# Regrouping channels by block copies from GpSimd's queue in the S5 and convolution mixer

## The chip, the cores and the metric
One core of one Trainium2 chip runs the whole kernel, a two-layer encoder trunk on 512 tokens of width 1024. The metric is the device time of one execution in microseconds (us), the median of several runs.

## The reference
Each layer is a mixer, a cross-attention and a gated FFN, each added to `h`. The change lies in the mixer of the second layer; the rest is the same. Cut to that:

```python
def s5_scan(u, ...):                       # u (B, S, G, Hc): 32 groups of 16 channels, 64 complex states
    bu_re = jnp.einsum('gph,bsgh->bsgp', bb_re, u)
    bu_im = jnp.einsum('gph,bsgh->bsgp', bb_im, u)
    _, _, s_re, s_im = lax.associative_scan(combine, (a_re, a_im, bu_re, bu_im), axis=1)
    return (jnp.einsum('ghp,bsgp->bsgh', c_re, s_re)
            - jnp.einsum('ghp,bsgp->bsgh', c_im, s_im))

def conformer_conv(h, conv_w, conv_b, ln_g, ln_b):
    val, gate = jnp.split(h, 2, axis=-1)
    u = depthwise_conv(val * jax.nn.sigmoid(gate), conv_w, conv_b)      # 31 taps
    return jax.nn.silu(layernorm(u, ln_g, ln_b))

def mixer_cd(hn, ...):
    u_c, h_d = split_sizes(hn @ w_in, (C_WIDTH, 2 * D_WIDTH))           # 512 and 2 x 512 channels
    u = u_c.reshape(Bn, S, C_NGROUPS, C_GROUP)
    y_f = s5_scan(u, ...); y_b = flip(s5_scan(flip(u), ...))
    z = jax.nn.gelu((y_f + y_b).reshape(Bn, S, C_WIDTH) + d_skip * u_c)
    o_c = z * jax.nn.sigmoid(z @ w_glu + b_glu)
    return jnp.concatenate([o_c, conformer_conv(h_d, ...)], axis=-1) @ w_out
```

## The kernel before
Activations lie with channels on the partitions: a tile is 128 channels by 512 steps. Projections are exact to f32: `mm3` (L206 to L208) runs three passes of 128x128 weights over 512 columns. Each weight block of 512 KB is loaded by SP (`wraw`, L147, three buffers `wr`), its high half made by ACT (`wh`, L201), its low half by DVE (`wl`, L202).

`mixer_cd` works on four blocks i = 0 to 3 of 128 channels, that is 8 groups each. Its stages and their letters:
- `u`, `v`, `g`: the projections to the scan's input, the convolution's value and its gate. `u_` evicts on DVE (L1327); the gate's product is L1447.
- `a`, `b`: `chunks` and `steps_` regroup a block. The 512 steps are 64 chunks of 8; eight transposes (L1336) put chunks on the partitions, ACT copies (L1337), eight more (L1345) put (step in chunk, channel of group) on the 128 partitions and (group, chunk) along the row, and ACT copies into `Rg` (L1353). `A`, `B` do the same for the convolution's input of the blocks 2 and 3, into `vg`.
- `l`, `L`, `m`, `w`: SP's loads of tables; `L` loads the two rotation tables `cst` of a block (L1363, two buffers, one for each direction).
- `c`, `C`: the scan of a block forward and backward: matmuls (L1374), ACT copy `T1` (L1377), two DMAs on SP that swap its halves (L1378, L1379), then on DVE the rotation (L1380 to L1382), the scan (L1384 or L1386) and the rotation back (L1387, L1388), whose last product frees the table's buffer.
- `s`, `x`, `y`: a second swap of halves on SP (L1394, L1395), the sum `xp` on DVE (L1402), and the output matmuls (L1416, L1418).
- `f`: `channels`, eight transposes (L1425) back to channels, the skip term on DVE (L1431, read with a stride from PSUM) and Gelu on ACT.
- `q`: two of the 30 taps of the convolution on DVE (L1463), for the blocks 0 and 1. For the blocks 2 and 3 `Z` does it by matmuls with tables (L1489), and `F` returns them by `channels` (L1497).
- `k`: a step of the next cross-attention's memory projections; `N` the sums of the layer norm.

The order of work is written out by hand in the string `CD` (L82 to L87), a letter and a block for each stage. `pinned` (L184) ties the first instruction of each stage on PE and on SP to that order; a scheduler places all else, so that the order on DVE follows from its choices:

```python
PS_ = (PE, nc.sync)
for st_ in CD.split():
    engs, fn = stage[st_[0]]
    pinned(engs, fn, int(st_[1]))
```

Of the kernel before, what the change touches and what calls it, by code (L numbers as in the profile page):

```python
# [90 lines left out]
def trunk(ctx, tc, xT, memT, pos, vec, amask, cmask, bmask,  # L91
# [1166 lines left out]
    def mixer_cd(norm, nnext, kv):  # L1258
# [70 lines left out]
        def chunks(src):  # L1329

            us = src.rearrange("p (c t) -> p t c", t=8)
            at = k4([64, 8, 8, 16], "at", 3)
            for hf in range(2):
                tp = tp_ps()
                for t in range(4):
                    PE.transpose(tp[:64, 128 * t:128 * t + 128], us[:, 4 * hf + t], ident)  # L1336
                A.activation(at[:, :, 4 * hf:4 * hf + 4].rearrange("c g t k -> c t g k"),  # L1337
                             tp[:64].rearrange("c (t g k) -> c t g k", t=4, k=16), AF.Copy)
            return at

        def steps_(at):

            rp = sc_ps()
            for g in range(8):
                PE.transpose(rp[:, 64 * g:64 * g + 64], at[:, g].rearrange("c t k -> c (t k)"), ident[:64, :64])  # L1345
            return rp
# [18 lines left out]
        def c_(i, d):  # L1365
# [44 lines left out]
        def y_(i):  # L1410
            At[i] = k4([64, 8, 8, 16], "at", 3)
            for hf in range(2):
                yp = sc_ps()
                for g in range(4):
                    o, gg = yp[:64, 128 * g:128 * g + 128], 4 * hf + g
                    PE.matmul(o, Rg[i][:, 64 * gg:64 * gg + 64], cm[i][0][:, gg], start=True, stop=False)  # L1416
                    for d in range(2):
                        PE.matmul(o, X[i, d][:, gg, d:d + 64], cm[i][1 + d][:, gg], start=False, stop=d == 1)  # L1418
                A.activation(At[i][:, :, 4 * hf:4 * hf + 4].rearrange("c t g k -> c g t k"),
                             yp[:64].rearrange("c (g t k) -> c g t k", g=4, k=16), AF.Copy)  # L1420

        def channels(at):
            yq = sc_ps()
            for t in range(8):
                PE.transpose(yq[:, 64 * t:64 * t + 64], at[:, t].rearrange("c g k -> c (g k)"), ident[:64, :64])  # L1425
            return yq

        def f_(i):
            us = uT[i].rearrange("p (c t) -> p t c", t=8)
            yq = channels(At[i])  # L1430
            V.scalar_tensor_tensor(us, us, vc("s5_d", i), yq.rearrange("p (t c) -> p t c", t=8),  # L1431
                                   op0=ALU.mult, op1=ALU.add)
            A.activation(uT[i], uT[i], AF.Gelu_apprx_tanh)

# [7 lines left out]
        def g_(i):  # L1442
            ps = half1(8 + i)
            g = b2("dg", 1)
            V.tensor_tensor(g, ps, R, ALU.mult)
            A.activation(g, g, AF.Tanh, scale=0.5)
            V.scalar_tensor_tensor(dv[i], g, 1.0, dv[i], op0=ALU.add, op1=ALU.mult)  # L1447

# [17 lines left out]
        def ca_(i):  # L1466
            Bt[i] = chunks(dv[i])

        def cb_(i):
            A.activation(vg[i % 2][:, :, 2:66], g3(steps_(Bt[i])), AF.Copy)  # L1470

# [10 lines left out]
        def z_(i):  # L1482
            hf = zs[i] = zs.get(i, -1) + 1
            if hf == 0:
                Bt[i] = k4([64, 8, 8, 16], "at", 3)
            yp, ts = sc_ps(), [cts.pop(0) for _ in range(2)]
            for g in range(4):
                for j in range(5):
                    PE.matmul(yp[:64, 128 * g:128 * g + 128], vg[i % 2][:, 4 * hf + g, j:j + 64], ts[g // 2][:, g % 2, j],  # L1489
                              start=j == 0, stop=j == 4)  # L1490
            A.activation(Bt[i][:, :, 4 * hf:4 * hf + 4].rearrange("c t g k -> c g t k"),
                         yp[:64].rearrange("c (g t k) -> c g t k", g=4, k=16), AF.Copy)

# [41 lines left out]

        PS_ = (PE, nc.sync)
        stage = {"u": (PS_, u_), "a": (PS_, a_), "b": (PS_, b_), "x": ((), x_), "y": (PS_, y_),
                 "l": (PS_, l_), "L": (PS_, r_), "m": (PS_, m_), "s": (PS_, s_),
                 "c": (PS_, lambda i: c_(i, 0)), "C": (PS_, lambda i: c_(i, 1)),
                 "f": (PS_, f_), "v": (PS_, lambda i: half0(4 + i)), "V": (PS_, v_),  # L1540
                 "g": (PS_, lambda i: half0(8 + i)), "G": (PS_, g_),
                 "A": (PS_, ca_), "B": (PS_, cb_), "w": (PS_, w_), "Z": (PS_, z_), "q": ((V,), q_), "F": (PS_, cf_), "N": (PS_, n_),
                 "k": (PS_, k_), "K": (PS_, lambda i: kv.load())}
# [102 lines left out]
def layout(inp):  # L1646
# [87 lines left out]
```

## Time and profile before

| | us |
|---|---|
| three runs: median (lowest to highest) | 1602.35 (1599.77 to 1603.43) |
| the profiled execution | 1605.85 |
| its span | 1604.1 |
| PE busy | 1558.4 (97%) |
| DVE busy | 1072.0 (67%) |
| ACT busy | 707.6 (44%) |
| GpSimd (POOL) busy | 327.3 (20%) |

The profile shows one execution. Its own time stands 1.75 us above its span and 3.5 us above the median of the runs. PE, DVE, ACT, POOL and SP are TensorE, VectorE, ScalarE, GpSimd and SyncE; SPq is SP's queue of DMAs. Busy shares over the whole span mix stages with different limits; the mixer in question lies between about 866 and 1110 us.

### The profile page before, as it was taken

Reading aid. Unit: us, or ns where it says so; the run is one execution under the profiler, and the core shown is the slowest. Engines: PE = TensorE matmul, PEld = TensorE weight load, DVE = VectorE, ACT = ScalarE, POOL = GpSimd, SP = SyncE. Lnnn points to the kernel's source line nnn. Section 1 sums busy time; section 2 is a strip of 40 time slices with the busy share of each in tenths; the row PEclk is TensorE's granted clock in tenths of the full one; section 3 lists DMA queues with packets and bytes.
Section 4 is the critical chain, followed back from the end, with each engine's and each line's share of the span. In section 5 each row is a group of like instructions: output and inputs, shape, how many; then the busy total and the mean of one; then the engine's idle time right before and its main releaser. Section 6 shows DMA issues by size and latency. Waiting matters only on the chain.

```text
span 1604.1 us, 20956 instructions
## 1 busy us (share of the span) xinstructions
PE 1558.4 (97%) x8036; PEld 1303.9 (81%) x8036; DVE 1072.0 (67%) x1492; ACT 707.6 (44%) x1089; POOL 327.3 (20%) x354
## 2 busy tenths in 40 slices
PE   9999999999999998998999998999999999999997
PEld 6787889888888776786788877888888888888887
DVE  7586766467568789479846797476646766636644
ACT  5464755355444344233336343374535444424423
POOL 8402000000049953553520000000000111100101
PEclk9999999999999999999999999999999999999998
DMA  5323333231222334544545666453202232332331
GB/s 179 109 65 94 110 114 106 79 118 57 76 73 94 120 116 122 168 125 128 149 151 202 210 223 224 157 184 107 90 27 92 94 103 93 96 101 92 95 104 65
DMA packets 76117, 189.11 MB, mean 118 GB/s; under 512 B 8368, under 2 KB 27440, under 8 KB 76016
## 3 DMA queue, kind: packets, MB, share of 16 engines
q1 hardware_dynamic: 75376, 186.58, 36.1%
q8 instruction: 63, 1.03, 0.3%
q0 software_dynamic: 320, 1.05, 0.2%
q14 instruction: 38, 0.31, 0.1%
q10 hardware_dynamic: 320, 0.13, 0.0%
HBM read 162.43 MB, written 19.01 MB: 113 GB/s over the span
## 4 chain that ended last, share of the span: by engine, by line
PE 70%; DVE 13%; POOL 6%; DMA 4%; ACT 3%; issue 3%; SPq 1%; ACTq 0%; DVEq 0%; POOLq 0%
PE mm L206 20%; PE mm L208 20%; PE mm L207 20%; DVE wl L202 2%; PE mm L737 2%; PE sc L1489 1%; DVE t L972 1%; DMA T1s<-T 1%; DVE t L971 1%; PE tp L724 1%; DVE t L976 1%; POOL t L1139 1%; PE sc L208 1%; PE sc L206 1%; PE sc L207 1%
## 5 line engine op out<-in xcount | busy, mean ns | idle before, releaser
L201 ACT ACTIVATE wh<-wr 128x1024 fp32r<-128x1024 f32 (+1 forms) x229 | 239.0, 1045 | 428.4 <-PE mm L207 311.3
L208 PE MATMUL mm<-hg,wl 128*128 128x512 f32 x1000 | 392.9, 393 | 15.9 <-DVE wl L202 15.9
L206 PE MATMUL mm<-hg,wh 128*128 128x512 f32 x1000 | 396.9, 397 | 1.3 <-ACT wh L201 1.3
L207 PE MATMUL mm<-hg,wh 128*128 128x512 f32 x1000 | 391.3, 391 | 0.0
L202 DVE TENSOR_TENSOR wl<-wr,wh 128x1024 fp32r<-128x1024 f32 (+1 forms) x229 | 296.2, 1294 | 76.4 <-ACT wh L201 74.4
L208 PEld LDWEIGHTS mm<-hg,wl 128*128 128x128 f32 x1000 | 189.0, 189 | 60.3 <-DVE wl L202 19.8
L206 PEld LDWEIGHTS mm<-hg,wh 128*128 128x128 f32 x1000 | 189.2, 189 | 42.9 <-issue 2.2
L207 PEld LDWEIGHTS mm<-hg,wh 128*128 128x128 f32 x1000 | 189.1, 189 | 39.5 <-issue 1.2
L976 POOL TENSOR_TENSOR t<-t,t 128x512 f32<-128x512 f32 x22 | 28.9, 1315 | 626.7 <-ACT t L182 622.7
L208 PE MATMUL mm<-g,wl 128*128 128x512 f32 x324 | 126.7, 391 | 2.7 <-DVE wl L202 2.7
L206 PE MATMUL mm<-g,wh 128*128 128x512 f32 x324 | 126.9, 392 | 0.0
L207 PE MATMUL mm<-g,wh 128*128 128x512 f32 x324 | 126.2, 389 | 0.0
L968 DVE TENSOR_TENSOR u<-mm,R 128x512 f32<-128x512 f32 x88 | 60.3, 687 | 74.2 <-PE mm L208 74.0
L970 ACT ACTIVATE t<-u,vt 128x512 f32<-128x512 f32 x88 | 70.8, 806 | 50.3 <-DVE u L968 50.2
L986 DVE TENSOR_TENSOR h<-mm,h 128x512 f32<-128x512 f32 x40 | 27.6, 691 | 87.8 <-PE mm L208 87.7
L972 DVE SCALAR_TENSOR_TENSOR t<-u,vt,t 128x511 f32<-128x511 f32 x88 | 78.5, 892 | 4.3 <-DMA dct<-tr 1.8
L971 DVE SCALAR_TENSOR_TENSOR t<-u,vt,t 128x511 f32<-128x511 f32 x88 | 75.4, 857 | 8.0 <-ACT t L970 8.0
L208 PEld LDWEIGHTS mm<-g,wl 128*128 128x128 f32 x324 | 60.8, 188 | 16.4 <-DVE wl L202 3.5
L182 ACT ACTIVATE t<-t 128x512 f32<-128x512 f32 x44 | 27.8, 633 | 104.2 <-DVE t L972 104.2
L207 PEld LDWEIGHTS mm<-g,wh 128*128 128x128 f32 x324 | 60.8, 188 | 12.6
L206 PEld LDWEIGHTS mm<-g,wh 128*128 128x128 f32 x324 | 60.9, 188 | 12.2
L279 DVE TENSOR_TENSOR h<-mm,h 128x512 f32<-128x512 f32 x32 | 21.7, 688 | 46.2 <-PE mm L208 46.2
(520 smaller groups left out, 2981.7 us busy)
## 6 DMA issues: line engine op xcount, KB each, us to landing
wr<-in_w_up SPq DMA_DIRECT2D x88, 512.0 KB
wr<-in_w_dn SPq DMA_DIRECT2D x32, 448.0 KB
wr<-in_w_ab SPq DMA_DIRECT2D x16, 512.0 KB
wr<-in_w_xv SPq DMA_DIRECT2D x16, 512.0 KB
wr<-in_w_xk SPq DMA_DIRECT2D x16, 512.0 KB
wr<-in_w_xq SPq DMA_DIRECT2D x16, 512.0 KB
wr<-in_w_xo SPq DMA_DIRECT2D x16, 512.0 KB
wr<-in_w_dn SPq DMA_DIRECT2D x16, 512.0 KB
```

Source lines behind the costliest of these rows:

```text
L182: tabbed(A.activation(dst, src, fn, **kw))
L201: A.activation(H[:, :n], raw[:, :n], AF.Copy)
L202: (eng or V).tensor_tensor(L[:, :n], raw[:, :n], H[:, :n].bitcast(F32), ALU.subtract)
L206: PE.matmul(ps, lH, rH, start=start, stop=False)
L207: PE.matmul(ps, lH, rL, start=False, stop=False)
L208: PE.matmul(ps, lL, rH, start=False, stop=stop)
L737: PE.matmul(onat[:, 64 * j:64 * j + 64], pt[:, 128 * jt:128 * jt + 128], va[:, jt, 64 * hd:64 * hd + 64], start=jt == 0, stop=jt == 3)
L968: V.tensor_tensor(u, ps, R, ALU.mult)
L970: A.activation(t, u, AF.Identity, scale=vc(f"cw{l}", 44 + i), bias=vc(f"cb{l}", i))
L971: V.scalar_tensor_tensor(t[:, 1:], u[:, :S - 1], vc(f"cw{l}", i), t[:, 1:], op0=ALU.mult, op1=ALU.add)
L972: V.scalar_tensor_tensor(t[:, :S - 1], u[:, 1:], vc(f"cw{l}", 88 + i), t[:, :S - 1], op0=ALU.mult, op1=ALU.add)
L976: (V if l == 0 else G).tensor_tensor(res[1], res[1], res[0], ALU.mult)
```

## The change
The 512 channels of the mixer are permuted on the host (within each block from (group, channel) to (channel, group)), with the weights, gains and biases that go with them. A block of a projection is evicted with its steps in the order (step in chunk, chunk). Then step t of all chunks, for one channel of every group, is one block of 16 partitions in the grouped layout, and regrouping is eight copies each way: `forth` (16x8x64, 32 KB) in stages `a` and `A`, `back` (128x64, 32 KB) in the new stages `e` and `E`. They take the place of `chunks`, `steps_` and `channels`; stages `b` and `B` go. The 96 copies and the 32 swaps of the scans are issued from GpSimd's queue, and `pinned` now ties that queue too. The matmuls y and z put the table in the place of the weights (128 columns) and stream 64 columns. `u_` and the gate product of the blocks 2 and 3 write with a stride; `f_` reads contiguous tiles, and its Gelu permutes and writes into `Rg`.

```diff
 CD = """
-l0 L0 K0 u0 v0 V0 g0 a0 G0 b0 k1 u1 c0 C0 m0 q0 k1 a1 v1 V1 l1 q0 q0 s0 L1 b1 k1 g1 G1 x0 q0 q0 c1 C1 k1 q0 u2 q0 y0
-l2 q0 q1 a2 q1 k1 s1 q0 f0 L2 q1 v2 m1 q0 V2 x1 b2 q1 q0 g2 q0 G2 q1 c2 C2 A2 k1 q0 q1 y1 q0 k1 m2 B2 w2 q1 u3 s2 L3 q0 q1
-f1 k1 l3 a3 q0 q1 x2 k1 b3 q1 v3 q0 V3 Z2 c3 C3 q1 y2 q1 g3 w2 q1 G3 k1 m3 q1 f2 A3 s3 q1 Z2 k1 w3 x3 F2 q1 B3
-k1 k1 y3 Z3 w3 k1 f3 k1 Z3 k1 F3 N0
+l0 L0 K0 u0 v0 V0 a0 g0 G0 k1 u1 c0 C0 m0 q0 k1 a1 v1 V1 l1 q0 q0 s0 L1 k1 g1 G1 x0 q0 q0 c1 C1 k1 q0 u2 q0 y0
+l2 q0 q1 k1 a2 q1 s1 q0 L2 q1 v2 m1 q0 V2 x1 e0 q1 q0 g2 q0 G2 q1 f0 c2 C2 k1 A2 q0 q1 y1 q0 k1 m2 w2 q1 u3 s2 L3 q0 q1
+k1 l3 a3 q0 q1 x2 k1 e1 q1 v3 f1 q0 V3 Z2 c3 C3 q1 y2 q1 g3 w2 q1 G3 k1 m3 A3 q1 s3 q1 Z2 k1 w3 E2 x3 q1
+k1 e2 F2 k1 y3 Z3 w3 k1 e3 f2 k1 Z3 k1 f3 E3 k1 F3 N0
 """
...
-            V.tensor_tensor(uT[i], ps, R, ALU.mult)
+            V.tensor_tensor(ct3(uT[i]), tc3(ps), tc3(R), ALU.mult)
...
+        def forth(dst, src):
+            for t in range(8):
+                G.dma_start(dst[16 * t:16 * t + 16], src[:, 64 * t:64 * t + 64])
+
+        def back(dst, src):
+            for t in range(8):
+                G.dma_start(dst[:, 64 * t:64 * t + 64], g3(src[16 * t:16 * t + 16]))
 
         def a_(i):
-            At[i] = chunks(uT[i])
-
-        def b_(i):
             Rg[i] = b2("Rg", 4)
-            A.activation(Rg[i], steps_(At[i]), AF.Copy)
+            forth(g3(Rg[i]), uT[i])
...
-            nc.sync.dma_start(t1s[0:64], t1[64:128])
-            nc.sync.dma_start(t1s[64:128], t1[0:64])
+            G.dma_start(t1s[0:64], t1[64:128])
+            G.dma_start(t1s[64:128], t1[0:64])
...
         def y_(i):
...
+            yp = sc_ps()
+            for g in range(8):
+                o = yp[:, 64 * g:64 * g + 64]
+                PE.matmul(o, cm[i][0][:, g], Rg[i][:, 64 * g:64 * g + 64], start=True, stop=False)
+                for d in range(2):
+                    PE.matmul(o, cm[i][1 + d][:, g], X[i, d][:, g, d:d + 64], start=False, stop=d == 1)
+            At[i] = b2("sh", 3)
+            A.activation(At[i], yp, AF.Copy)
+
+        def e_(i):
+            y = b2("sd", 2)
+            back(y, At[i])
+            At[i] = y
 
         def f_(i):
...
+            V.scalar_tensor_tensor(uT[i], uT[i], vc("s5_d", i), At[i], op0=ALU.mult, op1=ALU.add)
+            A.activation(Rg[i].rearrange("p (c t) -> p c t", t=8), uT[i].rearrange("p (t c) -> p c t", t=8),
+                         AF.Gelu_apprx_tanh)
...
+                Bt[i] = b2("sh", 3)
+                V.scalar_tensor_tensor(ct3(Bt[i]), tc3(g), 1.0, tc3(dv[i]), op0=ALU.add, op1=ALU.mult)
...
         def ca_(i):
-            Bt[i] = chunks(dv[i])
...
+            forth(vg[i % 2][:, :, 2:66], Bt[i])
...
-        PS_ = (PE, nc.sync)
...
+        PS_ = (PE, nc.sync, G)
```

The scheduler's order moves with it. On DVE, at block 2's scan (block c2; `T_1325` and `T1s_8015` are the forward direction's tiles, `T_1329` and `T1s_8038` the backward one's; `dv` with a `vt` operand is a conv tap), before:

```order
L1463 SCALAR_TENSOR_TENSOR dv_7841<-dv_7634,vt,dv_7841 128x502
L1380 TENSOR_TENSOR T_1325_8014<-T_1325_8014,cst_7899 128x512
L1381 TENSOR_TENSOR T1s_8015<-T1s_8015,cst_7899 128x512
L202 TENSOR_TENSOR wl_8162<-wr_7963,wh_8161 128x1024
L1463 SCALAR_TENSOR_TENSOR dv_7841<-dv_7634,vt,dv_7841 128x503
L1380 TENSOR_TENSOR T_1329_8037<-T_1329_8037,cst_7901 128x512
L1381 TENSOR_TENSOR T1s_8038<-T1s_8038,cst_7901 128x512
```

The two directions' first rotations stand close together there, the second with 34 taps of the mixer ahead of it. In the changed kernel the second direction's (`T_1317`, `T1s_7992`) stand 29 rows behind the first's, and the rows just ahead of it are:

```order
L247 TENSOR_TENSOR Rn_8074<-rn_1328_8075,rn_1329_8076 128x2
L1452 SCALAR_TENSOR_TENSOR dv_7809<-dv_7615,vt,dv_7809 128x509
L1452 SCALAR_TENSOR_TENSOR dv_7563<-dv_7424,vt,dv_7563 128x498
L1452 SCALAR_TENSOR_TENSOR dv_7809<-dv_7615,vt,dv_7809 128x510
L1452 SCALAR_TENSOR_TENSOR dv_7563<-dv_7424,vt,dv_7563 128x497
L1452 SCALAR_TENSOR_TENSOR dv_7809<-dv_7615,vt,dv_7809 128x511
L1370 TENSOR_TENSOR T_1317_7991<-T_1317_7991,cst_7854 128x512
L1371 TENSOR_TENSOR T1s_7992<-T1s_7992,cst_7854 128x512
```

Now 49 taps, 11 weight splits for 10 and five sums `xp` for four stand ahead of it; the first direction's has 35 taps ahead where it had 33.

On SP, around the tables of block 3 (`cst`) and the weights of v3 (`wr` from `in_w_cd`), before:

```order
L1394 DMA X2s_8195<-T1s_8038 64x512
L1395 DMA X2s_8195<-T1s_8038 64x512
L1363 DMA cst_8198<-dct_0_118 128x1024
L1363 DMA cst_8200<-dct_1_119 128x1024
L147 DMA wr_8217<-in_w_cd 128x1024
```

and in the changed kernel, where the swaps are on GpSimd's queue:

```order
L147 DMA wr_8096<-in_w_xv 128x1024
L1353 DMA cst_8135<-dct_0_118 128x1024
L1353 DMA cst_8137<-dct_1_119 128x1024
L147 DMA wr_8143<-in_w_cd 128x1024
L1348 DMA bm_8161<-dbm_0_102 128x1024
```

v3's weights stand directly behind the second table, which takes the buffer of the backward direction of c2.

On GpSimd's queue, at the swaps of block 3 (`T1s_8304` the backward direction's, `X2s` the second swaps) and the copies of `A3` (`vg`), in the changed kernel:

```order
L1368 DMA T1s_8304<-T_1368_8303 64x512
L1369 DMA T1s_8304<-T_1368_8303 64x512
L1385 DMA X2s_8423<-T1s_8281 64x512
L1335 DMA vg_7313<-sh_8385 16x8x64 x8
L1384 DMA X2s_8423<-T1s_8281 64x512
L1384 DMA X2s_8426<-T1s_8304 64x512
L1385 DMA X2s_8426<-T1s_8304 64x512
```

Three of block 3's four second swaps stand behind the eight copies; before, the four stood on SP with none ahead.

## Rows read from the trace of the kernel before

**Rows 1.** Page, part 1: busy us, share of the span, instructions
```profile
PE 1558.4 (97%) x8036; PEld 1303.9 (81%) x8036; DVE 1072.0 (67%) x1492; ACT 707.6 (44%) x1089; POOL 327.3 (20%) x354
```

**Rows 2.** Windows: stretch, length, busy by engine (instructions), PE clock, DMA share, GB/s
```profile
877.00:892.00 15.00, 14.75 (x94) 12.54 (x93) 10.15 (x19) 10.00 (x17) 0.00 (x0) 1.00 0.11 31
892.00:913.00 21.00, 21.00 (x115) 17.61 (x113) 18.46 (x28) 6.36 (x11) 0.00 (x0) 1.00 0.98 309
913.00:920.00 7.00, 5.98 (x54) 5.59 (x53) 5.99 (x9) 2.95 (x4) 0.00 (x0) 1.00 0.65 246
920.00:962.00 42.00, 41.14 (x249) 33.78 (x247) 41.73 (x66) 18.07 (x30) 0.00 (x0) 1.00 0.63 213
962.00:975.00 13.00, 8.21 (x31) 5.78 (x32) 11.64 (x18) 4.35 (x7) 0.00 (x0) 0.87 0.89 301
...
1005.00:1045.00 40.00, 40.00 (x310) 36.22 (x309) 18.72 (x24) 14.45 (x20) 0.00 (x0) 0.98 0.41 146
```

**Rows 3.** Waits of PE, 860 to 1110 us: total us, times, longest
```profile
PE mm L207 <- DVE wl L202: 4.7, 3, 2.5
PE mm L206 <- ACT wh L201: 2.3, 2, 1.2
```

**Rows 4.** Chain that ended last, 860 to 1110 us: start us, us, what
```profile
877.54 0.87 PE tp L1336 x8
...
881.15 0.64 PE sc L1345 x8
881.79 0.43 PE mm L206
882.22 0.23 PE mm L207
...
948.68 1.31 DVE dv L1463 x2
949.99 1.13 DVE wl L202
...
960.34 1.12 DVE uT L1431
961.46 0.61 DVE T1s L1388
...
964.17 0.33 SPq L1363
964.60 5.96 DMA wr<-in_w_cd
...
978.23 4.51 PE sc L1489 x40
982.74 3.73 PE tp L1374 x32
...
987.62 4.24 DMA T1s<-T
```

**Rows 5.** Timeline of PE: start us, us, engine, line, op, out<-in, xcount
```profile
965.88 0.79 PE L207 MATMUL mm<-wl,mg 128*128 128x512 f32 x1 [2.45 <-DVE wl L202]
...
969.03 0.44 PE L206 MATMUL mm<-wh,mg 128*128 128x512 f32 x1
...
971.69 0.50 PE L206 MATMUL mm<-hg,wh 128*128 128x512 f32 x1 [1.11 <-ACT wh L201]
...
1019.84 0.43 PE L1416 MATMUL sc<-cm,Rg 128*64 128x128 f32 x2
```

**Rows 6.** GpSimd's DMAs, line 793 alone: ns min/median/max, starts; landing
```profile
L793 POOL DMA_DIRECT2D h<-in_xT x4: 536/542/743, 260.1 to 288.8; - x4
...
DMA to landing us min/median/max: 2.7/3.5/4.5
```

**Rows 7.** Timeline of DVE around g3's gate product
```profile
1003.63 0.69 DVE L1447 SCALAR_TENSOR_TENSOR dv<-dg,dv 128x512 f32<-128x512 f32 x1
```

**Rows 8.** Waits of SP's queue, 860 to 1065 us: total us, times, longest
```profile
SPq L1378 <- ACT T L1377: 38.8, 5, 18.1
```

More of the change, by code (lines that the diff above doesn't have):

```diff
@@ L1270, in mixer_cd @@
         g3 = lambda v: v.rearrange("p (g c) -> p g c", c=64)
+        tc3 = lambda v: v.rearrange("p (c t) -> p t c", t=8)
+        ct3 = lambda v: v.rearrange("p (t c) -> p t c", t=8)
         xp = [T.tile([128, 8, 65], F32, name=f"xp{j}") for j in range(2)]
@@ L1326, in u_ @@
             uT[i] = b2("uT", 4)
-            V.tensor_tensor(uT[i], ps, R, ALU.mult)
[L1329 to L1346, printed above, removed]
+            V.tensor_tensor(ct3(uT[i]), tc3(ps), tc3(R), ALU.mult)
[5 more added lines that the diff above has]
+                G.dma_start(dst[:, 64 * t:64 * t + 64], g3(src[16 * t:16 * t + 16]))
         def a_(i):
-            At[i] = chunks(uT[i])
-        def b_(i):
             Rg[i] = b2("Rg", 4)
-            A.activation(Rg[i], steps_(At[i]), AF.Copy)
+            forth(g3(Rg[i]), uT[i])
         def l_(i):
@@ L1393, in s_ @@
                 xs, t1s = b2("X2s", 2), X[i, d][1]
-                nc.sync.dma_start(xs[0:64], t1s[64:128])
-                nc.sync.dma_start(xs[64:128], t1s[0:64])
+                G.dma_start(xs[0:64], t1s[64:128])
+                G.dma_start(xs[64:128], t1s[0:64])
                 X[i, d] = X[i, d][0], xs
@@ L1410, in y_ @@
         def y_(i):
[L1411 to L1426, printed above, removed]
-        def f_(i):
[L1429 to L1433, printed above, removed]
+            yp = sc_ps()
[10 more added lines that the diff above has]
+            At[i] = y
+        def f_(i):
+            V.scalar_tensor_tensor(uT[i], uT[i], vc("s5_d", i), At[i], op0=ALU.mult, op1=ALU.add)
+            A.activation(Rg[i].rearrange("p (c t) -> p c t", t=8), uT[i].rearrange("p (t c) -> p c t", t=8),
+                         AF.Gelu_apprx_tanh)
         dv = {}
@@ L1446, in g_ @@
             A.activation(g, g, AF.Tanh, scale=0.5)
-            V.scalar_tensor_tensor(dv[i], g, 1.0, dv[i], op0=ALU.add, op1=ALU.mult)
+            if i < 2:
+                V.scalar_tensor_tensor(dv[i], g, 1.0, dv[i], op0=ALU.add, op1=ALU.mult)
+            else:
+                Bt[i] = b2("sh", 3)
+                V.scalar_tensor_tensor(ct3(Bt[i]), tc3(g), 1.0, tc3(dv[i]), op0=ALU.add, op1=ALU.mult)
         accs, cts, Bt, zs, done = {}, [], {}, {}, {}
@@ L1484, in z_ @@
             if hf == 0:
-                Bt[i] = k4([64, 8, 8, 16], "at", 3)
+                Bt[i] = b2("sh", 3)
             yp, ts = sc_ps(), [cts.pop(0) for _ in range(2)]
@@ L1488, in z_, with ce_ @@
                 for j in range(5):
-                    PE.matmul(yp[:64, 128 * g:128 * g + 128], vg[i % 2][:, 4 * hf + g, j:j + 64], ts[g // 2][:, g % 2, j],
+                    PE.matmul(yp[:, 64 * g:64 * g + 64], ts[g // 2][:, g % 2, j], vg[i % 2][:, 4 * hf + g, j:j + 64],
                               start=j == 0, stop=j == 4)
-            A.activation(Bt[i][:, :, 4 * hf:4 * hf + 4].rearrange("c t g k -> c g t k"),
-                         yp[:64].rearrange("c (g t k) -> c g t k", g=4, k=16), AF.Copy)
+            A.activation(Bt[i][:, 256 * hf:256 * hf + 256], yp[:, :256], AF.Copy)
+        def ce_(i):
+            y = b2("sd", 2)
+            back(y, Bt[i])
+            Bt[i] = y
         def cf_(i):
-            yq = channels(Bt[i])
             accs[i] = b2("dv", 6)
-            A.activation(accs[i].rearrange("p (c t) -> p t c", t=8), yq.rearrange("p (t c) -> p t c", t=8),
+            A.activation(accs[i].rearrange("p (c t) -> p c t", t=8), Bt[i].rearrange("p (t c) -> p c t", t=8),
                          AF.Identity, bias=vc("conv_b", i))
@@ L1534, in k_ @@
                 tabset("gelu_apprx_tanh_and_others", True)
-        PS_ = (PE, nc.sync)
-        stage = {"u": (PS_, u_), "a": (PS_, a_), "b": (PS_, b_), "x": ((), x_), "y": (PS_, y_),
+        PS_ = (PE, nc.sync, G)
+        stage = {"u": (PS_, u_), "a": (PS_, a_), "e": (PS_, e_), "x": ((), x_), "y": (PS_, y_),
                  "l": (PS_, l_), "L": (PS_, r_), "m": (PS_, m_), "s": (PS_, s_),
@@ L1541, in mixer_cd @@
                  "g": (PS_, lambda i: half0(8 + i)), "G": (PS_, g_),
[L1542 removed]
+                 "A": (PS_, ca_), "E": (PS_, ce_), "w": (PS_, w_), "Z": (PS_, z_), "q": ((V,), q_), "F": (PS_, cf_), "N": (PS_, n_),
                  "k": (PS_, k_), "K": (PS_, lambda i: kv.load())}
@@ L1551, in mixer_cd @@
         for i in range(4):
-            split(hg[i], uT[i])
+            split(hg[i], Rg[i])
         for i in range(4):
@@ L1561, in mixer_cd @@
             tact(sgm, ps, AF.Tanh, scale=0.5, bias=bgh[:, i:i + 1])
-            V.scalar_tensor_tensor(sgm, sgm, 1.0, uT[i], op0=ALU.add, op1=ALU.mult)
-            o_t[i] = k4([128, 2, S], "at" if i < 2 else "bm", 3 if i < 2 else 2, F32R)
+            V.scalar_tensor_tensor(sgm, sgm, 1.0, Rg[i], op0=ALU.add, op1=ALU.mult)
+            o_t[i] = k4([128, 2, S], "ct" if i < 2 else "bm", 2, F32R)
             A.activation(o_t[i][:, 0], sgm, AF.Copy, scale=0.5)
@@ L1653, in layout @@
     p = np.arange(128)
+    q = np.arange(512).reshape(4, 8, 16).transpose(0, 2, 1).reshape(512)
     parts = {"g_final": _col(f("g_final")), "gla_bg": _col(f("gla_bg")[0]), "gla_norm": _col(f("gla_norm")[0]),
-             "s5_d": _col(f("s5_d")[0]), "s5_bg": _col(f("s5_b_glu")[0]), "conv_w": _col(f("conv_w")[0]),
-             "conv_b": _col(f("conv_b")[0]), "ln_g": _col(f("conv_ln_g")[0]), "ln_b": _col(f("conv_ln_b")[0]),
+             "s5_d": _col(f("s5_d")[0][q]), "s5_bg": _col(f("s5_b_glu")[0][q]), "conv_w": _col(f("conv_w")[0][:, q]),
+             "conv_b": _col(f("conv_b")[0][q]), "ln_g": _col(f("conv_ln_g")[0][q]),
+             "ln_b": _col(f("conv_ln_b")[0][q]),
              "invf": invf[p % 32].reshape(128, 1), "rsign": np.where(p % 64 < 32, -1.0, 1.0).reshape(128, 1),
@@ L1689, in layout @@
     a["wg2"] = g2
-    a["w_cd"] = _blocks(f("w_in_cd")[0])
-    a["w_glu"] = _blocks(f("s5_w_glu")[0])
-    a["w_ocd"] = _blocks(f("w_out_cd")[0])
+    a["w_cd"] = _blocks(f("w_in_cd")[0][:, np.concatenate([q, 512 + q, 1024 + q])])
+    a["w_glu"] = _blocks(f("s5_w_glu")[0][q][:, q])
+    a["w_ocd"] = _blocks(f("w_out_cd")[0][np.concatenate([q, 512 + q])])
     lre, lim = (f(n)[0].reshape(64, 64).T for n in ("s5_lam_re", "s5_lam_im"))
```

2 lines of the change are left out of this document (removed).

## The prediction

> **What bounds the kernel now.** I read four things in turn: busy shares of the whole span, then busy time by stretch inside the second mixer (866 to 1110 us of the span), then the waits of TensorE in it, then the chain that ended last. TensorE (PE) is busy for 97% of the span [rows 1], so in general a microsecond of PE work that goes is a microsecond of time. The stretches show where this fails [rows 2]: from 920 to 962 us PE and VectorE (DVE) are both full, 41.14 and 41.73 of 42 us, while from 1005 to 1045 us PE alone is full (40.00 of 40, DVE 18.72). Behind the full DVE, from 962 to 975 us, PE does 8.21 us of work in 13, at a mean clock of 0.87: the place where a late DVE costs time. The waits name it: projections wait 4.7 us for the low weight halves that DVE makes (L202) and 2.3 us for the high halves of ScalarE (ACT, L201) [rows 3]. The chain tells why: c2's last rotation product on DVE ends at 961.46 + 0.61 = 962.07 us, behind conv taps, a weight split and two evictions; with it the buffer of the rotation table comes free, SyncE (SP) issues the next table and only behind it v3's weights, which land 5.96 us later [rows 4]. v3's first matmul starts at 971.69 us [rows 5]. So what decides in this mixer is when c2's second direction is through DVE.
>
> **TensorE's gain.** Six chunk transposes, six step transposes and six channel transposes go. Eight chunk transposes took 0.87 us; eight step transposes 0.64 us, and the projection matmul behind them 0.43 instead of the 0.23 us of its neighbours, so 0.84 us; channel transposes have the same shape. 6 x (0.87 + 0.84 + 0.84) = 15.3 us. The output matmuls y and z change to the form of the scan's input matmuls: 16 of those took 3.73 us (0.233 each), 20 of z took 4.51 (0.2255) [rows 4]. 96 of y and 80 of z, 0.0077 more each: +1.4 us. That is 13.9 us less PE work. Of it, four channel, one step and one chunk set stand behind v3: 4 x 0.84 + 0.84 + 0.87 = 5.1 us, less 128 matmuls x 0.0077 = 1.0, so **4.1 us** count. The other 9.8 us lie ahead of v3, in the stretch where DVE and v3's weights set the end; there they become waiting, and I count nothing. The ACT copies out of PSUM that go end none of PE's waits [rows 3], so nothing either.
>
> **DVE up to c2's last product.** The order rows show 15 more conv taps ahead of the second direction's rotation than before (49 for 34): two taps took 1.31 us, so 15 x 0.655 = 9.83. One more weight split, 1.13; one more sum xp, two tiles like L1388's contiguous product, 0.61. Three operations with a stride now (u2, u3, one gate product): no row shows exactly these; the nearest is the strided eviction into uT, 1.12 against 0.61, so 0.51 each and 1.53 in all (bounds: 0 and 0.6 each). Of two strided evictions in f one remains ahead, contiguous: 2 x 1.12 - 0.61 = 1.63 saved [rows 4]. Sum: 9.83 + 1.13 + 0.61 + 1.53 - 1.63 = +11.5 us. DVE has some room behind 892 us: 2.54 + 1.01 + 0.27 = 3.8 us [rows 2] that the earlier taps may fill, so the bounds are +7.7 and +11.8. I take +11.5, since the order puts the taps where DVE was full. c2's last product then ends at 973.6 us.
>
> **From there to v3.** On SP the swaps no longer stand ahead of the tables: the table is issued at once (0.33 us), v3's weights start at 974.0. Landing: 5.96 us with two tables just ahead, now one; a quarter-megabyte load alone landed in 2.7 us [rows 4, 6]. I take 4.7 us, nearer the upper row, because the same traffic surrounds it (bounds 2.7 and 5.96). ACT's half took 971.69 - 970.56 = 1.1 us up to the matmul. v3 starts at 974.0 + 4.7 + 1.1 = 979.8, **+8.1 us** (+2.3 to +9.7 with all bounds).
>
> **After v3.** The transposes that go: -4.1. PE has then stood still for about 9 us. After the 2.45 us wait of before, matmuls started 0.43 us apart (half the clock) from 965.88 to 969.03, 3.1 us for work of 1.6 [rows 5]; that again at v3: +1.5 (bounds 0 and 3). Then GpSimd's queue: x3's last three swaps now stand behind the eight copies of A3. These wait for g3's gate product, which ended at 1003.63 + 0.69 = 1004.3 us [rows 7], so at 1012.9 with the shift and a stride. Eleven issues at 0.54 us [rows 6] are 5.9 us, to 1018.8; a swap's landing was 4.24 us [rows 4], two sums 1.2: 1024.2. y3 stood at 1019.84 [rows 5]; shifted by 8.1 and 1.5, less 3.4 of transposes, 1026.0, or 3.7 earlier if PE's later waits for low halves (4.7 - 2.5 = 2.2 us [rows 3]) and 1.5 of half clock vanish. Wait: 0 to 1.9, with landings as slow as 5.96 us up to 3; I take +1. E3's eight copies at the end, 8 x 0.54 + 2.7 = 7.0 us, lie beside the gated output projection: nothing, at most +3.
> Sum: 8.1 - 4.1 + 1.5 + 1.0 = **+6.5 us**. The profiled execution took 1605.85 us, 3.5 above the median of 1602.35; 1605.85 + 6.5 = 1612.35, and against the median **1608.9 us**. With the terms' bounds: +0.7 to +13, so 1603 to 1615.
>
> **GpSimd's queue and the rule on it.** The only DMAs that GpSimd issues before are four, of 256 KB: 0.536 to 0.743 us each, landing after 2.7 to 4.5 us [rows 6]. 128 more at 0.54 are 69 us in a mixer of some 200, on an engine that stood empty there (POOL 0.00 in every stretch of [rows 2]): hidden, but for x3. By these rows eight copies in a row have landed some 7 us after the first issue.
>
> **Rivals.** (1) **Faster.** DVE's free time takes up the earlier taps, and SP, no longer held by swaps (38.8 us of waits for ACT [rows 8]), issues weights early, so that the PE gain counts in full and part of the 7.0 us of waits [rows 3] goes too: 1602.35 - 13.9 = 1588 (1584 with 4 us of waits gone, 1597 with some 40% of the gain). It decides by whether c2's last product ends before about 965 us. Against it: DVE's 41.73 of 42 us, and the table's buffer, which is still freed by that product. 0.16. (2) **GpSimd's queue is the bound.** Not 0.54 but 1.2 us for a DMA among busy engines: 128 x 0.66 = 84 us more on the queue. On the path stand the 11 of x3 (7.3 us) and E3's eight (5.3): 12.6 on top of 6.5, about 1621; at 1.5 us a DMA 1627. The isolated issues speak against it; that nothing shows an issue beside a full DVE speaks for it. 0.14. The Trainium skill's page "SBUF — State Buffer", section "SBUF: two separate sides", has this as a rule: a DMA issued from GpSimd's queue gets its descriptors written there, and while VectorE runs an operation in a two-port mode GpSimd cannot write them, so the transfer seems blocked by VectorE. By that rule an operation with two SBUF inputs locks only against reads by GpSimd, so conv taps and rotations would not stop these copies and the sum stands; no run here shows either. (3) **No net change**: the tap delay is half absorbed and PE's 4.1 us and part of the earlier gain balance it, about 1602. 0.10.
>
> **How the numbers follow.** Forecast 0.60, of which some 0.05 lies under 0.2% (3.2 us, about what a measurement of this kernel can tell from no change). So faster by over 0.2% 0.16, within 0.2% 0.15, slower 0.69. The range must leave out two in ten: it reaches down to 1594, into rival 1 (0.10 left out), and up to 1627, over most of rival 2 (some 0.05 left out).
>
> **What would show it.** Right: in the changed profile c2's second last-product (L1378) ends near 973 us, the weights of v3 are issued behind the table just after, PE waits about 9 us ahead of v3, and PE's rows for the mixer hold 14 us less work. Wrong: no wait ahead of v3 and PE full from 920 us on (rival 1); or DMA issues on POOL above 1 us each and PE's waits ending with xp sums or copies instead of weights (rival 2).

## The result and the profile after

| | us |
|---|---|
| changed kernel, 4 runs: median (lowest to highest) | 1639.36 (1636.96 to 1649.40) |
| kernel before, 4 runs beside them | 1601.06 (1597.09 to 1603.43) |
| ratio, 95% interval | 1.0237 [1.0208, 1.0265] |
| profiled execution: span | 1635.5 |

The change costs 38 us. In the profiled executions the span grew by 31.4 us. The page's first part of the changed kernel, which answers to [rows 1]:

```profile
PE 1561.9 (95%) x7892; PEld 1310.3 (80%) x7892; DVE 1073.0 (66%) x1492; ACT 697.3 (43%) x1067; POOL 395.8 (24%) x482
```

PE holds 144 instructions fewer, yet is busy for 3.5 us more: if 13.9 us of work went, as my sum had it, the rest ran 17.4 us slower, an estimate by difference. Its idle time, span less busy, grew from 45.7 to 73.6 us, by 27.9. The two growths, 27.9 and 3.5, make up the 31.4 us. The waits of PE between 860 and 1150 us (total us, times, longest) show where it stands, beside [rows 3]:

```profile
PE mm L206 <- ACT wh L201: 15.4, 2, 8.7
PE sc L1406 <- issue: 10.3, 2, 7.8
PE mm L207 <- DVE wl L202: 4.1, 2, 3.2
PE sc L1406 <- DVE xp L1392: 2.9, 2, 2.6
```

With three smaller ones they sum to 35.5 us, against 8.7 before. "issue" at L1406 is the first matmul of y0 that needs a sum `xp`. The windows (columns as in [rows 2]) show the other half, the clock:

```profile
913.00:920.00 7.00, 0.41 (x2) 0.30 (x2) 2.49 (x4) 2.49 (x3) 4.60 (x9) 0.64 1.04 308
920.00:945.00 25.00, 23.27 (x96) 20.69 (x97) 24.38 (x37) 3.98 (x5) 8.09 (x16) 0.69 0.69 196
...
962.00:985.00 23.00, 12.15 (x40) 8.52 (x38) 21.25 (x37) 5.92 (x11) 8.66 (x17) 0.74 0.63 196
985.00:1000.00 15.00, 9.46 (x32) 7.23 (x32) 4.25 (x5) 3.92 (x4) 0.00 (x0) 0.60 0.74 247
1000.00:1020.00 20.00, 20.00 (x148) 18.71 (x148) 8.52 (x12) 4.86 (x8) 2.07 (x4) 1.00 0.70 224
...
1040.00:1060.00 20.00, 18.26 (x85) 18.26 (x86) 3.13 (x4) 3.17 (x5) 8.34 (x17) 0.53 0.35 64
```

From 913 to 945 us, from 962 to 1000 us and from 1040 to 1060 us the granted clock is far below full, to 0.53; before, the lowest stretch of [rows 2] had 0.87. The timeline of PE has the places:

```profile
913.52 0.41 PE L1406 MATMUL sc<-xp,cm 128*128 128x64 f32 x2 [2.52 <-issue]
921.73 0.66 PE L1406 MATMUL sc<-xp,cm 128*128 128x64 f32 x2 [7.81 <-issue]
...
974.97 1.22 PE L206 MATMUL mm<-wh,mg 128*128 128x512 f32 x2 [6.67 <-ACT wh L201]
...
990.50 0.79 PE L206 MATMUL mm<-hg,wh 128*128 128x512 f32 x1 [8.73 <-ACT wh L201]
...
999.27 4.57 PE L1475 MATMUL sc<-vg,ct 128*128 128x64 f32 x40
...
1041.74 0.69 PE L1406 MATMUL sc<-xp,cm 128*128 128x64 f32 x2 [2.62 <-DVE xp L1392]
...
1051.18 8.74 PE L1475 MATMUL sc<-vg,ct 128*128 128x64 f32 x40
...
1061.53 0.40 PE L208 MATMUL mm<-mg,wl 128*128 128x256 f32 x1
1061.75 0.30 PE L206 MATMUL mm<-mg,wh 128*128 128x256 f32 x1
```

PE waits 2.52 and 7.81 us in y0, where I had expected nothing; 6.67 us for weights of the memory projections, which I had not expected either; 8.73 us ahead of v3, where I had some 9; and 2.62 us in y3. After that wait y3 and the first half of z3 (1051.18) run at half clock, PE fully busy, and so does what follows, 20 us in all: the 40 matmuls of z take 8.74 us instead of the 4.57 of z2 (999.27), and only some 2 us into the projections behind them the time from one matmul to the next halves (1061.75).

GpSimd's issues took what [rows 6] showed, 0.52 to 0.68 us each, and fill less than half of all but one of the windows above (POOL); so it is not the queue's rate. Their landing is another matter. Two swaps of the changed kernel from issue to landing, at 952.3 and 913.1 us, and the windows around each, whose second last column is the DMA share:

```profile
DMA to landing us min/median/max: 2.3/2.3/2.3
...
DMA to landing us min/median/max: 6.2/6.2/6.2
```

```profile
952.00:954.00 2.00, 1.79 (x11) 1.40 (x9) 2.00 (x4) 0.53 (x2) 1.36 (x3) 1.00 0.32 66
...
913.00:915.00 2.00, 0.41 (x2) 0.30 (x2) 1.07 (x2) 0.00 (x0) 1.85 (x4) 1.00 1.06 248
```

2.3 us where the DMA engines stand a third busy, 6.2 where they are full; SP's swap of [rows 4] took 4.24.

What makes y0 late is seen on three engines. On SP (timeline; a duration that spans a wait includes it):

```profile
906.92 1.65 SPq L1353 DMA_DIRECT2D cst<-dct  x2
908.66 0.43 SPq L147 DMA_DIRECT2D wr<-in_w_xv  x1
...
965.84 17.11 SPq L1353 DMA_DIRECT2D cst<-dct  x2
983.04 0.38 SPq L147 DMA_DIRECT2D wr<-in_w_cd  x1
```

On DVE (with the second rotation and the last product of c2, for below):

```profile
907.53 0.69 DVE L1378 TENSOR_TENSOR T1s<-T1s,cst 128x512 f32<-128x512 f32 x1
...
912.74 0.68 DVE L1392 TENSOR_TENSOR xp<-T,X2s 128x512 f32<-128x512 f32 x1
...
918.37 1.23 DVE L202 TENSOR_TENSOR wl<-wr,wh 128x1024 fp32r<-128x1024 f32 x1 [4.30 <-ACT wh L201]
919.80 1.23 DVE L202 TENSOR_TENSOR wl<-wr,wh 128x1024 fp32r<-128x1024 f32 x1 [0.21 <-ACT wh L201]
920.95 0.68 DVE L1392 TENSOR_TENSOR xp<-T,X2s 128x512 f32<-128x512 f32 x1
...
974.01 0.67 DVE L1370 TENSOR_TENSOR T<-T,cst 128x512 f32<-128x512 f32 x1
...
981.93 0.67 DVE L1378 TENSOR_TENSOR T1s<-T1s,cst 128x512 f32<-128x512 f32 x1
```

In the kernel before, c0's last rotation product on DVE, and the projection weights on SP:

```profile
901.45 0.69 DVE L1388 TENSOR_TENSOR T1s<-T1s,cst 128x512 f32<-128x512 f32 x1
```

```profile
904.43 0.43 SPq L147 DMA_DIRECT2D wr<-in_w_xv  x1
```

The scan's first swap is issued at 892.26 instead of 889.85 us, behind seven copies of `a1`, and DVE has v1's eviction and a weight split ahead of the rotation now, so c0's last rotation product ends at 908.2 instead of 902.1 us. The table on SP waits for it, and the projection weights stand behind the table: issued at 908.66 instead of 904.43. DVE has those weights' split ahead of the second sum `xp` in its order: it idles 4.30 us, and PE 7.81. The split is only half of that wait. The last swap for this sum was issued at 909.02 us, and its time to landing was

```profile
DMA to landing us min/median/max: 8.0/8.0/8.0
```

so the sum could have started at 917.0 instead of 920.95: some 4 us of the wait are the splits', the rest is the swap itself, issued late and slow to land.

The same comes again at the table of block 3: it blocks SP for 17.11 us until c2's last product (982.6, where I had 973.6), v3's weights start at 983.04, and v3 stands at 990.50 instead of 971.69. DVE is busy for 21.25 of the 23 us from 962 to 985, and c2's second rotation starts at 974.01 though its last swap, issued at 957.92, had landed 3.0 us later: here it is DVE's work that stands ahead. What that work is worth, e3 and e9 show. y3's 2.62 us are a split again, ahead of the second sum:

```profile
1039.86 1.23 DVE L202 TENSOR_TENSOR wl<-wr,wh 128x1024 fp32r<-128x1024 f32 x1 [2.10 <-ACT wh L201]
1041.00 0.68 DVE L1392 TENSOR_TENSOR xp<-T,X2s 128x512 f32<-128x512 f32 x1
```

The last of x3's swaps, issued at 1035.27 behind the copies of A3, had landed 2.2 us later.

### The profile page after: what moved, and what is told of

Read it like the earlier page. It is cut to its first block, busy times and chain, and to the rows that moved or that the text cites. A ratio compares the mean times of both kernels' runs of the same rounds, so it can differ in the third digit from the quotient of the medians.

```text
span 1635.5 us, 20813 instructions
## 1 busy us (share of the span) xinstructions
PE 1561.9 (95%) x7892; PEld 1310.3 (80%) x7892; DVE 1073.0 (66%) x1492; ACT 697.3 (43%) x1067; POOL 395.8 (24%) x482
```

## The experiments

| run | median us | ratio to before, 95% |
|---|---|---|
| e1 swaps back on SP | 1612.02 | 1.0044 [1.0020, 1.0068] |
| e2 before, swaps on GpSimd | 1617.62 | 1.0061 [1.0030, 1.0092] |
| e3 taps behind c2's rotation | 1638.67 | 1.0199 [1.0172, 1.0227] |
| e4 projection between y3 and z3 | 1640.04 | 1.0200 [1.0157, 1.0242] |
| e5 tables behind weights | 1627.20 | 1.0111 [1.0074, 1.0149] |
| e6 before, tables behind weights | 1599.92 | 0.9963 [0.9936, 0.9991] |
| e7 swaps on SP, tables behind weights | 1606.08 | 1.0000 [0.9974, 1.0025] |
| e8 y, z with 128 columns streamed | 1620.84 | 1.0085 [1.0057, 1.0112] |
| e9 16 tap stages late | 1637.76 | 1.0217 [1.0183, 1.0251] |
| e10 e7 with taps late | 1604.46 | 0.9992 [0.9968, 1.0015] |
| e11 e6 with taps late | 1602.22 | 0.9998 [0.9975, 1.0021] |
| e12 tables on GpSimd | 1613.57 | 1.0042 [1.0022, 1.0062] |
| e13 before, y3 held | 1620.87 | 1.0087 [1.0055, 1.0119] |
| e14 e13 with 64 columns | 1627.89 | 1.0113 [1.0081, 1.0145] |
| e15 e10 with tables on GpSimd | 1613.12 | 1.0030 [1.0005, 1.0055] |

The kernel before stood at 1604.88 to 1605.87 us beside them, 1601.06 beside the changed kernel; so the ratios are what to set against its 1.0237. The mixer does not begin at the same time in every trace: where two traces are compared below, times are counted from the first eviction of u on DVE (before 876.55 us, changed kernel 876.60).

**e1 and e2: whose queue the swaps are on.** e1 is the changed kernel with

```diff
-            G.dma_start(t1s[0:64], t1[64:128])
-            G.dma_start(t1s[64:128], t1[0:64])
+            nc.sync.dma_start(t1s[0:64], t1[64:128])
+            nc.sync.dma_start(t1s[64:128], t1[0:64])
```

and the same for `X2s`; e2 makes the opposite edit in the kernel before.

> The changed kernel with the 32 swaps of the scans issued by SyncE again; the 96 copies stay on GpSimd. In its order c2's second rotation has 15 conv taps fewer ahead of it than in the changed kernel. Theory A (the swaps on GpSimd's queue, behind copies, and the DVE order that follows from them cost the time): v3's first matmul comes back from 990 to 970 to 978 us, PE's wait ahead of y0 from 10.3 to under 3 us, time 1595 to 1612 us. Theory B (the 96 copies, landing in 5 us each, are what is late): v3 stays behind 985 us, time 1625 to 1640. Theory C (matmuls of y and z with 64 streamed columns leave the clock at half once PE has waited): y3 and z3 at half clock again only if PE waits just ahead of y3; without such a wait they run at full clock.

> The kernel before with only the 32 swaps moved to GpSimd's queue; transposes as before, no copies. c2's second rotation has 2 conv taps more ahead of it than before. Theory A in its strong form (a swap on GpSimd's queue is slow by itself): +8 to +20 us, 1609 to 1621. Theory A in its weak form (slow only behind copies and by the DVE order that they bring): 1599 to 1607 us. Theory B: no change, 1599 to 1604.

e1: 1612.02 us, at the edge of theory A's range, ratio 1.0044 for 1.0237; y0's wait is gone, v3 stands at 978.42, and y3 and z3, with no wait ahead, run at full clock. So the copies alone, with the PE work that they save, cost some 0.4%, and theory B falls. e2: +0.6%, about 10 us, with nothing but the swaps moved. The timelines of e2, DVE and PE:

```profile
899.43 0.69 DVE L1380 TENSOR_TENSOR T<-T,cst 128x512 f32<-128x512 f32 x1 [7.14 <-DMA T1s<-T]
```

```profile
922.51 1.86 PE L1418 MATMUL sc<-cm,xp 128*64 128x128 f32 x6 [6.06 <-issue]
```

DVE waits 7.14 us for the first swap, 3.34 before. The swaps were issued no later than before: the first at 892.82, 13.6 us behind the first eviction of u (879.21 here), for 13.3. But SP, which no longer stops at the swaps, had issued two tables of 512 KB at 891.92 us, ahead of them; before, the next loads followed at 892.79, behind the swaps. The first pair of swaps landed 5.0 and 5.9 us after its issue; before, DVE went on 2.5 us after the second of the pair was issued (890.44). y0 waits 6.06 us here too, without a copy in the kernel. The time is that of theory A's strong form; that the loads ahead make the swap slow, and not GpSimd's queue as such, rests on the landings (2.3 and 6.2 us above, and e12), for no run moves those loads alone.

**e3 and e9: the conv taps on DVE.** e3 ties all taps written behind c2 behind its second rotation (an ordering edge from that rotation's first product to each such tap). e9 moves 16 of the `q` tokens ahead of `v3` in the order string behind it.

> The changed kernel with the conv taps that are written behind c2 in the order string tied behind c2's second rotation on DVE: 34 taps ahead of it as in the order string, 11 fewer than in the changed kernel. All queues as in the changed kernel. If the DVE order alone makes c2 late: c2's last product ends some 11 x 0.655 = 7 us earlier, near 975 us, v3 near 983, time 1629 to 1634. If the swap's landing behind seven copies is the limit: DVE waits ahead of the rotation instead, c2 ends within 3 us of before, time 1636 to 1643.

> The changed kernel with 16 of the tap stages (32 of 60 taps) moved in the order string from ahead of v3 to behind it, where DVE is half empty; queues as in the changed kernel. c2's second rotation then has 20 taps ahead of it instead of 45 (counted for both blocks). If DVE's taps are what makes c2 and v3 late (the step of the prediction): v3's first matmul comes 15 us or more earlier, near 972 us, time 1615 to 1625. If it is the chain of waits through the queues (swap on GpSimd, last rotation, table, weights, weight half, sum xp) that y0 has too: y0's wait stays near 10 us, v3 gains under 8 us, 1630 to 1640.

Neither gains clear of the noise: 1638.67 and 1637.76 us, ratios 1.0199 and 1.0217 for 1.0237, with intervals that overlap. In e9 (SP, DVE and PE timelines) DVE reaches the rotation early and then stands:

```profile
966.85 0.61 SPq L144 DMA_DIRECT2D wr<-in_w_xv  x1
967.56 17.21 SPq L1350 DMA_DIRECT2D cst<-dct  x2
984.86 0.38 SPq L144 DMA_DIRECT2D wr<-in_w_cd  x1
```

```profile
970.96 0.68 DVE L1367 TENSOR_TENSOR T<-T,cst 128x512 f32<-128x512 f32 x1
971.56 0.68 DVE L1368 TENSOR_TENSOR T1s<-T1s,cst 128x512 f32<-128x512 f32 x1
979.40 1.23 DVE L199 TENSOR_TENSOR wl<-wr,wh 128x1024 fp32r<-128x1024 f32 x1 [7.16 <-ACT wh L198]
...
983.72 0.69 DVE L1375 TENSOR_TENSOR T1s<-T1s,cst 128x512 f32<-128x512 f32 x1
```

```profile
992.13 0.80 PE L203 MATMUL mm<-hg,wh 128*128 128x512 f32 x1 [7.65 <-ACT wh L198]
```

The second rotation begins at 970.96 us, behind an eviction, with DVE otherwise empty; the first eviction of u stands at 880.25 in this trace, so that is 6.7 us earlier in the work than the 974.01 of the changed kernel. Next in DVE's order is a weight split (979.40), whose weights SP issued at 966.85, here not behind a table but behind five loads for y and z; DVE waits 7.16 us inside the rotation (e3: 6.20 at the same split). So c2's last product ends at 984.4, only 1.8 us earlier in the work than in the changed kernel, the table on SP waits for it (17.21), and PE 7.65 us for v3's weights. 25 taps, some 16 us of DVE's time at 0.655 each, were worth 1.8 us: behind them stood another wait of much the same length.

**e5, e6, e7, e12: the tables on SP.** e5 writes stage `L` later, behind the next weights:

```diff
-... s0 L1 k1 g1 G1 x0 ... s1 q0 L2 q1 v2 m1 ... s2 L3 q0 q1 k1 l3 a3 ...
+... s0 k1 g1 L1 G1 x0 ... s1 q0 q1 v2 L2 m1 ... s2 q0 q1 k1 L3 l3 a3 ...
```

e6 does it in the kernel before, e7 with e1's edit. e12 instead takes the tables off SP:

```diff
-                nc.sync.dma_start(rot[i, d], d_ct[i][d])
+                G.dma_start(rot[i, d], d_ct[i][d])
```

> The changed kernel with the loads of the rotation tables (stage L of the blocks 1 to 3) written one or two stages later in the order string, behind the next projection's weights on SyncE's queue; all copies and swaps stay on GpSimd. The DVE order moves too: c2's second rotation has 13 taps fewer ahead of it than in the changed kernel. Theory D (a table that waits on SyncE for DVE's last rotation product holds the weights behind it, and PE waits for those): PE's waits for weight halves ahead of v3 fall from 6.7 and 8.7 us to under 3 each, y0's wait from 10.3 to under 5, time 1606 to 1622. If the landing of GpSimd's transfers sets the end (theory A or B), the waits only move to y0 to y3 and the scans: 1630 to 1640.

> The kernel before with the same three stages moved: a control for e5. Theory D: PE's wait of 1.1 us ahead of v3 and part of the 7 us for weight halves go, 1594 to 1601 us. Otherwise 1600 to 1606.

> The changed kernel with both: swaps on SyncE, tables behind the weights. If the two effects add (A and D) and nothing but the 14 us of PE work less is left: 1588 to 1598 us, faster than before. If the copies are late by themselves (B): PE waits ahead of the scans' matmuls or y remain, 1600 to 1612.

> The changed kernel with the loads of the rotation tables issued from GpSimd's queue, just behind the second swaps, which wait for the same rotation products; so no weight stands behind a table on SyncE any more. Theory D (SyncE holds the weights behind a table that waits for DVE): PE's waits for weight halves ahead of v3 fall from 15.4 us to under 7, y0's wait from 10.3 to under 4, time 1608 to 1622. If the weights' landing in the traffic and the swaps' landing set the end: the waits stay, 1628 to 1640.

e5: 1627.20, less than theory D wanted. v3 no longer waits, but the weights after the next still stand behind a table, and y0 waits 5.79 and 6.55 us. e12, where no weights do, answers: 1613.57 us, ratio 1.0042 for 1.0237, in theory D's range, though all 128 transfers, and eight tables more, are on GpSimd's queue. Its waits of PE (860 to 1150 us):

```profile
PE sc L1406 <- issue: 6.5, 2, 5.9
PE mm L207 <- DVE wl L202: 6.4, 1, 6.4
PE mm L206 <- ACT wh L201: 6.0, 2, 5.1
```

Nothing is listed ahead of v3. The second swaps landed in 3.4 us (median), for 5.6 in the changed kernel. But y0 still waits 6.5 us, where theory D wanted under 4: that wait does not need a table on SP. e12's DVE order moved as well (33 taps ahead of c2's second rotation for 45), but e3 and e9 moved that much and gained nothing clear. e6 shows that the table held the kernel before a little, too: 0.9963, the fastest kernel here. e7 comes out level with before, not faster as theories A and D together wanted: PE's waits there are 17.8 us (e6: 4.9), so about what went of PE's work is still waited for.

**e10, e11, e15: where the gain of PE went.** e10 is e7, e11 is e6, each with e9's late taps; e15 is e10 with e12's edit in the place of e5's.

> e7 (swaps on SyncE, tables behind the weights, copies on GpSimd) with the same 16 tap stages behind v3. If the 14 us of PE work less were lost in e7 because DVE was full ahead of v3: PE's waits fall from 17.8 to under 9 us, 1594 to 1600 us, faster than before. If the copies' and weights' landing holds PE: waits stay above 13 us, 1603 to 1608.

> e6 (the kernel before with the tables behind the weights) with 16 tap stages behind v3, a control for e10. Little is left to win there, PE waits only 4.9 us in e6: 1596 to 1601.

> The changed kernel with swaps on SyncE, tables on GpSimd's queue, copies on GpSimd, and 16 tap stages behind v3. If the table on SyncE is what still holds e10's weights (6.5 us ahead of v3): 1592 to 1600 us, faster than before. If what holds them is the order of big loads on SyncE (y's tables and z's tables ahead of them): as e10, 1601 to 1608.

e10: 1604.46, not faster, against the theory that DVE's taps ate the gain. The largest wait left, 6.49 us at 970, is for memory weights that stand on SP behind the loads for y and z; e15 has it too (7.27), with no table on SP, and so has the changed kernel (6.67). e15's time, 1613.12, lies above both of its ranges; what its further cost is stays open. So loads are what PE reaches earlier now and waits for; I did not try another order of those loads, so that stays argued. e11 gained nothing over e6.

**e4, e8, e13, e14: the form of y and z.** e4 writes `k1` between y3 and z3. e8 gives y and z of the changed kernel back the form of before, data as weights and 128 table columns streamed; its results lie in other places. e13 holds y3 in the kernel before, by copying the tile of its last swap there and back four times, and e14 is e13 with the changed kernel's form (results in other places again):

```diff
+                if (i, d) == (3, 1):
+                    for _ in range(4):
+                        G.dma_start(t1s, xs)
+                        G.dma_start(xs, t1s)
```

> The changed kernel with one projection step (512 streamed columns) moved from ahead of y3 to between y3 and the first half of z3. Theory C: y3 still starts at half clock, but the projection lifts it, the first half of z3 takes 4.5 instead of 8.7 us, time 1633 to 1636 if y3's wait stays at 2.6 us. If the clock comes back by time alone: z3 at half clock as before, no gain, 1637 to 1642; as y3 stands earlier, its wait for the xp sums may grow by up to the step's 2.7 us.

> The changed kernel with y and z in the form of the kernel before: 64 columns of data as weights, 128 columns of the table streamed. The result lies in other places, so what follows computes on misplaced values; the work and its order by data are the same. DVE's order moves with it (16 taps fewer ahead of c2's second rotation). Theory C (the clock does not rise while 64 columns are streamed): after any wait ahead of y the clock is back within some 5 us, inside y; no stretch of 18 us at half clock at y3 and z3; with the two waits gone or not, the time at half clock falls by 15 us or more, which is worth 7 us or more. If it comes back no sooner than in the changed kernel, theory C falls.

> The kernel before with block 3's last second swap followed by eight more copies of that tile (four times there and back, 256 KB each, one waiting for the other), so that y3's last sum comes late and PE waits some 8 us ahead of the first matmul of y3 that needs it; y and z with 128 streamed columns. Theory C: the clock falls to half in that wait and is back within 5 to 6 us of the restart, inside y3; time before + wait + 2 to 3 us.

> e13 with y and z in the changed kernel's form, 64 streamed columns against 128-column table weights (results in other places, what follows computes on misplaced values). Theory C: after the same wait y3 and the first half of z3 stay at half clock until a projection with 256 or 512 columns has run, some 10 to 18 us, so 3 to 7 us more than e13. If the form does not matter: within 2 us of e13 (its matmuls at full clock cost 1.4 us more in all).

The waits came out longer than meant, 13.80 and 11.63 us. PE's timeline in e13 after the wait, and in e14:

```profile
1028.29 0.69 PE L1422 MATMUL sc<-cm,xp 128*64 128x128 f32 x2 [13.80 <-DVE xp L1406]
...
1031.75 0.93 PE L1422 MATMUL sc<-cm,xp 128*64 128x128 f32 x6
1032.52 0.38 PE L1420 MATMUL sc<-cm,Rg 128*64 128x128 f32 x2
```

```profile
1032.40 0.69 PE L1421 MATMUL sc<-xp,cm 128*128 128x64 f32 x2 [11.63 <-DVE xp L1406]
...
1041.85 8.74 PE L1493 MATMUL sc<-vg,ct 128*128 128x64 f32 x40
...
1051.99 0.41 PE L207 MATMUL mm<-mg,wh 128*128 128x256 f32 x1
...
1052.37 0.28 PE L206 MATMUL mm<-mg,wh 128*128 128x256 f32 x1
```

With 128 columns streamed the time from one matmul to the next halves inside y3, some 4 us after the restart (1032.52); with 64, y3 and all of the first half of z3 run at 1.2 GHz, and the clock rises at 1052.37, 20 us after the restart, behind projections with 256 columns. The times, 1620.87 and 1627.89, lie 7 us apart with a wait 2 us shorter in e14, though their intervals overlap; the rows decide it. e8 agrees: after a wait of 6.94 us ahead of y0 full pace was back 3 us later, and in y3, after waits of 1.40 and 1.09 us, 3 us after the second; from 1040 to 1060 us the clock was 1.00 where the changed kernel had 0.53. The form changes two things at once, 64 streamed columns for 128 and weights of 128 columns for 64; which of them holds the clock down is not separated. e8's 1620.84 is no price of the form alone, as DVE's order moved with it. e4 came out inconclusive: the projection changed PE's order, z2's second half (not z3) then followed a 2.49 us wait and ran at half clock.

## Why the prediction was wrong

Forecast 1608.9 us, range up to 1627; measured 1639.36. The direction was right. In the profiled executions v3 came 18.8 us later, where I had 8.1, and what lies behind v3 took 12.6 us more, where I had 1.6 less.

- **The failed step: "DVE up to c2's last product".** I read the order rows, 15 taps more ahead of the rotation, as most of 11.5 us of lateness. The traces hold 45 taps there for 27 (my counts, 49 and 34, were off), and c2's last product came 20.5 us later. But the taps are not what decides: e3 and e9 take 11 and 25 of them away, and c2's last product comes 2.6 us later and 1.8 earlier in the work. c2 is late because of a ring that I had only at its last link: swap on GpSimd, rotation, table on SP waiting for it, weights behind the table (or, in e9, behind the loads for y and z), their split ahead of the next product or sum on DVE. It turns once per block, and I priced one turn. Opened at the swaps (e1) or at the tables (e12), it gives back most of the loss: 1.0237 falls to 1.0044 or 1.0042. What to see was in the rows of SP's order: only the swaps, by waiting there, had kept the loads behind them.
- **y0.** I set no wait there; it was 10.3 us. The order of DVE showed a weight split ahead of the second sum `xp`, and I had taken DVE's idle time before 920 us as room. The split makes some 4 us of it; the rest is the swaps' late issue and landing, and 6.5 us stay in e12.
- **The memory weights ahead of v3.** I set no wait more there; it was 6.67 us.
- **v3**: a wait of 9 us forecast, 8.73 measured, for the reason given (table, then weights). That the numbers agree is luck: c2's last product came 9 us later than I had it, and PE reached v3 about as much later.
- **y3**: +1 us forecast, 2.62 measured, but for another reason: not x3's swaps behind the copies, but a weight split ahead of the sum.
- **The clock**: sized at 1.5 us from the one short stretch of [rows 5], all of it in matmuls with 512 columns; 17.4 us by difference. Some 8 of them are y3 and the first half of z3: 17.9 us from 1041.74 to 1059.68, where y2 took 5.3 and half of z2 4.4. I changed the form of y and z in the sum (+1.4 us at full clock) and did not ask what that form does behind a wait.
- **PE's work**: 13.9 us less stays my sum; no row gives it directly, and z at full clock did not get longer (4.57 us for 40 matmuls, 4.58 before), so it may be about 1 us too small. That what lies ahead of v3 becomes waiting held in e7 and e10 (17.8 and 16.5 us of waits).
- **The bounds**: the terms' own bounds add up to -1.8 and +14.6 us, not to +0.7 and +13; the measured +38 lies far outside both.
- **Rival 2** had the side and half the size, 1621 to 1627, by another cause: the issues took 0.52 to 0.68 us, not 1.2, beside a DVE that was full. The Trainium skill's rule in "SBUF — State Buffer", section "SBUF: two separate sides", that VectorE's two-port operations hold up a transfer from GpSimd's queue, was not what happened here: the conv taps and rotations beside the issues have two SBUF inputs, no issue took longer than 0.68 us, and the swap at 952.3 landed in 2.3 us beside a DVE busy for 2.00 of 2 us.

## What to carry to other kernels

Before a transfer that waits is moved off a queue, ask what stood behind it there: here its wait had kept other loads out of its way, and what waited next on that queue (the table, 17.11 us) held what stood behind. Count a saving on the bounding engine only where nothing else ends last. And a kernel whose matmuls come to stream fewer columns should be priced behind a wait as well as at full clock.

## What the hardware showed unexpectedly

After a wait, matmuls that stream 64 columns against weights of 128 stayed at 1.2 GHz with PE busy throughout, and the clock rose only behind projections with 256 columns, 20 us after the restart (the changed kernel from 1041.74, e14 from 1032.40); the same products with 128 columns streamed against weights of 64 were back at 2.4 GHz some 4 us after the restart (e13). Behind full-clock work the same 64-column matmuls ran at full clock: z2 and y2 of the changed kernel between 1000 and 1020 us, at 1.00. And GpSimd issued transfers at 0.52 to 0.68 us each beside a full DVE; what varied was the landing of a swap, 2.3 us at a DMA share of 0.32 and 6.2 at 1.06.
